# A hybrid convolution and state-space layer on one core: the last convolved tiles stay in SBUF, and the group norms are taken from four rows of 128

## The chip, the cores and the metric

The kernel runs on one core of one Trainium2 chip. The time is the device time of one execution in microseconds (us); several executions are timed and the median is given. The engines are PE (TensorE, matrix products), DVE (VectorE), ACT (ScalarE), POOL (GpSimd) and SP (SyncE, whose queue issues most DMAs; GpSimd and ACT issue DMAs on queues of their own). Each engine works through its instructions in a fixed order and waits on semaphores. The order is made when the kernel is built: a planner goes through the instructions with a priority for each (mainly its place in the program, shifted by hand with `tc.high_priority`) and with durations of its own, and writes one list for each engine.

## What is computed

One decoder layer on 1024 positions with 1024 channels, in float32. The part that matters here is the first sublayer, the mixers:

```python
h = layer_norm(x, ln_in_g, ln_in_b)
u = h @ w_in            # conformer GLU | z | x,B,C | dt | gate_a | gate_b
v = a * sigmoid(g);  v = causal_dwconv(v, 31 taps)        # conformer branch
y_a = silu(layer_norm(v)) @ w_conv_out
y   = SSD(silu(causal_dwconv(x,B,C)), dt) + x * d_skip     # Mamba-2 branch, 4 groups
yg  = y * silu(z)
yg  = yg * rsqrt(mean(yg**2 over the 512 channels of a group) + eps)
y_b = (yg * norm_w) @ w_ssm_out
h = layer_norm(alpha*h + (sigmoid(gate_a)*y_a + sigmoid(gate_b)*y_b) @ w_o)
h = layer_norm(alpha*h + conv_ffn(h))
```

Two normalisations are touched by the change: the norm over the 1024 channels of the convolved `v` (eight tiles of 128 channels), and the norm over the 512 channels of each of four groups of the state-space branch.

## The kernel before

Activations lie with channels on the 128 partitions and positions along the row. The sequence is worked in two halves of 512 positions, so a tile is 128 x 512. Float32 products are made from a high and a low part: a weight tile is loaded by SP into `st`, ACT casts the high part (L141), DVE subtracts to get the low part (L142), and each block takes three products (L153, L154, L155). One column of 128 channels is 8 blocks, 24 products (`project`). PSUM has eight banks, four (`acc`) for the projections and four (`sm`) for the rest.

For each half, `mixers` runs over four groups. For group g it projects the columns of B and C and four of x, each followed by a short convolution on DVE (`conv4`, L391); four z columns (`z_gate`); and two pairs of conformer columns (`glu`), which give two tiles `v`. Then `ssd_group` does the state-space part in four chunks of 128 positions: transposes (L478), decay factors on ACT (L485, L492), GpSimd's product `ce` (L496), products for the outputs (L517 and L520), the gate (L543), squares on ACT (L545), and DVE's sum of squares over the four tiles of a chunk into `ssum` (L546).

The function `scaled` makes the norm of one group: a product of `ssum` with a 128 x 128 matrix of ones (L553) gives every partition the sum over channels, ACT takes the square root (L554), DVE the reciprocal (L555) on 128 x 512, and four DVE instructions multiply `xT` by weight and norm (L558). The function `parts` splits the result into high and low parts in `yT` (L571 on ACT, L572 on DVE), which the output projection `ssm_out_first` (first half of the channels, eight columns) and the second half in `combine` use. The tiles `xT` have two buffers (`x4`), `ssum`, `rstd` and `ce` one each.

Meanwhile `conv31` convolves the two tiles `v` of the group with 31 taps: ACT starts each accumulator `c` (L425, two buffers), and DVE adds 30 taps to each, 60 instructions for a group (L436). It has a low priority (an offset of -1500), so its taps fill DVE wherever nothing more urgent is ready. Both accumulators then go to device memory (L445).

In the fourth group the first half of the output projection comes before the last splits. At the end of `mixers` eight gate columns are projected and stored. `combine` projects the other gates and the second half of the output projection (16 columns in turn), and, with a raised priority, does the conformer norm: SP loads the eight convolved tiles back (L655), GpSimd adds them (L660, L662), PE makes the mean by a product with a constant matrix (L664), then come differences (L667), squares (L669, L672), GpSimd's sum of these (L673), a second product (L675), and the normalised tiles for the last projection `wconv`. SP's queue holds the stores L445, the loads L655, the loads of the other branch `yb` (L643) and the weight loads (L139) in one line.

After `combine` of the second half come the output projection and the feed-forward part, about 700 us, which the change doesn't touch.

Of the kernel before, what the change touches and what calls it, by code (L numbers as in the profile page):

```python
# [55 lines left out]
def kernel(  # L56
# [31 lines left out]
    def bank(which):  # L88
        n_ps[0] += 1
        pl, tag = (pacc, "acc") if which else (psm, "sm")  # L90
        return pl.tile([P, 512], F32, tag=tag, name=f"{tag}{n_ps[0]}")
# [37 lines left out]
        [dram.tile([P, T], F32, name=f"{n}_scr{k}") for k in range(NK)] for n in ("b2", "t32")  # L129
    )  # L130
    acs_scr = [dram.tile([P, P], F32, name=f"acs_scr{i}") for i in range(2)]
    c_scr = [dram.tile([8, P, HALF], F32, name=f"c_scr{i}") for i in range(2)]
    g_scr = [dram.tile([8, P, HALF], F32, name=f"g_scr{i}") for i in range(2)]
    y_scr = [dram.tile([8, P, HALF], F32, name=f"y_scr{i}") for i in range(2)]
# [12 lines left out]
    def big_tile(name):  # L147
        return big.tile([P, 2, KD, HALF], F32R, tag="big", name=name)
# [255 lines left out]
    def glu(pl, hh, hT, i):  # L404
        pa, pg = bank(1), bank(1)
        wa = weights(wcol[CT_A + i], f"ga{hh}_{i}")
        project(pa, wa, hT)
        wg = weights(wcol[CT_G + i], f"gg{hh}_{i}")
        project(pg, wg, hT)
        v = pl.tile([P, HALF + KC - 1], F32, tag="v", bufs=4, name=f"v{hh}_{i}")  # L410
        s = pl.tile([P, HALF], F32, tag="sig", name=f"sig{hh}_{i}")
        A.activation(out=s, in_=pg, func=AF.Sigmoid)
        A.copy(v[:, : KC - 1], v_halo[:, i, :])
        V.tensor_mul(v[:, KC - 1 :], pa, s)
        if hh == 0:
            A.copy(v_halo[:, i, :], v[:, HALF:])
        return v

    def conv31(pl, hh, vs):

        accs = {}
        for i, v in vs:
            wc = PC_CW + i * KC
            c = pl.tile([P, HALF], F32, tag="c", bufs=2, name=f"c{hh}_{i}")
            A.activation(  # L425
                out=c,
                in_=v[:, KC - 1 :],
                func=AF.Identity,
                scale=pc[:, wc + KC - 1 : wc + KC],
                bias=pc[:, PC_CB + i : PC_CB + i + 1],  # L430
            )
            accs[i] = c
        for k in range(KC - 1):
            for i, v in vs:
                wc = PC_CW + i * KC
                V.scalar_tensor_tensor(  # L436
                    out=accs[i],
                    in0=v[:, k : k + HALF],
                    scalar=pc[:, wc + k : wc + k + 1],
                    in1=accs[i],  # L440
                    op0=ALU.mult,
                    op1=ALU.add,
                )
        for i, _ in vs:
            SY.dma_start(c_scr[hh][i], accs[i])  # L445

    def z_gate(pl, hh, hT, g):

# [5 lines left out]
    def ssd_group(pl, hh, g, xT, BT, CT, zs):  # L454
# [10 lines left out]
        for c in range(4):  # L465
# [67 lines left out]
            for i in range(4):  # L533
# [9 lines left out]
            V.tensor_mul(xT[:, :, cs], xT[:, :, cs], zs[:, :, cs])  # L543
            sq = pl.tile([P, 4, P], F32, tag="sq", name=f"sq{nm}")
            A.activation(out=sq, in_=xT[:, :, cs], func=AF.Square)  # L545
            V.tensor_reduce(  # L546
                out=ssum[:, cs], in_=sq.rearrange("p i l -> p l i"), axis=AX.X, op=ALU.add
            )

        def scaled():  # L550
            rstd = pl.tile([P, HALF], F32, tag="rstd", name=f"rstd{hh}_{g}")
            pv = bank(0)
            TE.matmul(pv, ones, ssum, start=True, stop=True)  # L553
            A.activation(out=rstd, in_=pv, func=AF.Sqrt, bias=eps, scale=1.0 / HALF)  # L554
            V.reciprocal(out=rstd, in_=rstd)  # L555
            for i in range(4):
                k = PC_NW + 4 * g + i
                V.scalar_tensor_tensor(  # L558
                    out=xT[:, i, :],
                    in0=xT[:, i, :],  # L560
                    scalar=pc[:, k : k + 1],
                    in1=rstd,
                    op0=ALU.mult,
                    op1=ALU.mult,
                )
# [12 lines left out]
    def ssm_out_first(pl, hh, yT):  # L578
        for j in range(8):
# [4 lines left out]
            A.copy(y, ps)  # L584
            SY.dma_start(y_scr[hh][j], y)

    def mixers(hh, hT):
        pre = first_columns(hh, hT, (CT_B, CT_C, CT_X))
        with pool(f"mixers{hh}") as pl:
            time_steps(pl, hh, pre[0])  # L590
            for g in range(GROUPS):
                BT = conv4(pl, hh, column(hh, hT, CT_B + g) if g else pre[1], 16 + g)
                CT = conv4(pl, hh, column(hh, hT, CT_C + g) if g else pre[2], 20 + g)
                xT = pl.tile([P, 4, HALF], F32, tag="x4", bufs=2, name=f"x4_{hh}_{g}")
                for i in range(4):
                    j = 4 * g + i
                    conv4(pl, hh, column(hh, hT, CT_X + j) if j else pre[3], j, xT[:, i, :])
                zs = z_gate(pl, hh, hT, g)
                vs = [(i, glu(pl, hh, hT, i)) for i in (2 * g, 2 * g + 1)]
                scaled, parts = ssd_group(pl, hh, g, xT, BT, CT, zs)  # L600
                if g == 2:
                    scaled()
                    split_2 = parts
                elif g == 3:
                    ssm_out_first(pl, hh, yT)
                    yT = big_tile(f"yT{hh}_{g}")
                    split_2(yT)
                    scaled()
                    parts(yT)
                else:  # L610
                    if g == 0:
                        yT = big_tile(f"yT{hh}_{g}")
                    scaled()
                    parts(yT)
                with tc.high_priority(offset=-1500):
                    conv31(pl, hh, vs)
            for j in range(8):
                pg = bank(1)
                project(pg, weights(wcol[CT_GA + j], f"gt{hh}_{j}"), hT)
                ga = pl.tile([P, HALF], F32, tag="ya", bufs=2, name=f"gt{hh}_{j}")  # L620
                A.activation(out=ga, in_=pg, func=AF.Sigmoid)
                SY.dma_start(g_scr[hh][j], ga)
        return yT

    def combine(hh, hT, yT):

        with pool(f"comb{hh}") as pl:
            mb, gbs = [], []
# [21 lines left out]
            with tc.high_priority(offset=900):  # L650
                cs = []
                for i in range(8):
                    if i % 2 == 0:
                        pair = pl.tile([P, 2, HALF], F32, tag=f"c{i // 2}", name=f"cc{hh}_{i}")
                    SY.dma_start(pair[:, i % 2, :], c_scr[hh][i])  # L655
                    cs.append(pair[:, i % 2, :])
# [462 lines left out]

    warm(75)  # L1120
    hT = ln_in_first()
    yT = mixers(0, hT)
    mixT, hT = combine(0, hT, yT)
    with pool("rows0") as pl:
        rs = [pl.tile([P, D], F32, name=f"r0_{t}") for t in range(4)]
        out_proj(pl, rs, 0, mixT)
        for t in range(4):
            SY.dma_start(h1_scr[t * P : (t + 1) * P, :], rs[t])
    yT = mixers(1, hT)
    state_stack.close()  # L1130
    mixT, _ = combine(1, hT, yT)
    ffn_stack = ExitStack()
    qp = ffn_stack.enter_context(pool("ffq", side="right"))
    with pool("trans") as tp:
# [118 lines left out]
```

## Time and profile before

| | us |
|---|---|
| median of three runs | 2007.0 (2004.78 to 2007.89) |
| the profiled execution | 2003.94 |
| its span, from the first to the last instruction | 2001.9 |
| PE busy | 1938.3 |
| DVE busy | 1697.2 |
| ACT busy | 1088.9 |
| GpSimd busy | 199.2 |

Busy time of PE counts products from start to modelled end, and since these overlap, a busy PE isn't always one that advances at its best rate. A wait in the views is the idle time of one engine in front of an instruction, put down to the engine or DMA that ended it. Tiles are named as in the program, without buffer numbers; `acc` and `sm` are PSUM banks.

### The profile page before, as it was taken

The numbers are of one execution on the slowest core, as the hardware profiler recorded it, in microseconds if no ns is written. First come the engines' busy times: TensorE is split into PE (matmuls) and PEld (weight loads), VectorE is DVE, ScalarE is ACT, GpSimd is POOL, SyncE is SP. The second block draws the span as 40 slices with busy tenths as digits, with TensorE's granted clock in tenths as the row PEclk, the third lists the DMA queues.
The fourth block names the chain that finished last, engine by engine and source line by source line (L and its number), as shares of the span: only waits on it lengthen the run. The fifth ranks groups of instructions, "written<-read, shape, count | busy, mean of one in ns | idle before, by whom it ended". The sixth has DMA issues, their size and how long they took to land.

```text
span 2001.9 us, 25547 instructions
## 1 busy us (share of the span) xinstructions
PE 1938.3 (97%) x9405; PEld 1578.4 (79%) x9405; DVE 1697.2 (85%) x2256; ACT 1088.9 (54%) x1619; POOL 199.2 (10%) x230
## 2 busy tenths in 40 slices
PE   9999999999699999999999979999999999989997
PEld 8888888777588788887777768888888888868886
DVE  7599999999695669999999977578788888869778
ACT  4676768553263266776685426355555555544432
POOL 0001010110410000101011022001000000121010
PEclk9999999999899999999999999999999999999999
DMA  5333333334465432323234353476455555578663
GB/s 216 110 97 109 105 101 111 115 132 138 142 223 169 161 108 98 108 99 106 92 120 137 118 168 126 134 278 240 152 168 195 174 179 179 174 278 310 195 227 126
DMA packets 110237, 311.20 MB, mean 155 GB/s; under 512 B 12832, under 2 KB 13344, under 8 KB 110112
## 3 DMA queue, kind: packets, MB, share of 16 engines
q1 hardware_dynamic: 91872, 256.61, 38.4%
q0 software_dynamic: 11904, 41.43, 5.9%
q10 hardware_dynamic: 6336, 11.54, 1.6%
q8 instruction: 74, 1.21, 0.2%
q14 instruction: 51, 0.42, 0.1%
HBM read 255.39 MB, written 54.13 MB: 155 GB/s over the span
## 4 chain that ended last, share of the span: by engine, by line
PE 53%; DVE 32%; DMA 6%; issue 5%; ACT 2%; POOL 1%; SPq 0%; DVEq 0%; ACTq 0%; POOLq 0%
DVE c L436 12%; PE acc L155 11%; PE acc L154 11%; PE acc L153 11%; PE sm L154 5%; PE sm L155 5%; PE sm L153 5%; DVE w_c L142 2%; DVE x L391 2%; DMA dr<-wdown 2%; DVE w_dn L1041 1%; DVE m L512 1%; DMA dr<-b_scr 1%; DVE x L535 1%; DVE xbc L391 1%
## 5 line engine op out<-in xcount | busy, mean ns | idle before, releaser
L436 DVE SCALAR_TENSOR_TENSOR c<-v,pc,c 128x512 f32<-128x512 f32 x480 | 364.2, 792 | 3.6 <-ACT c L425 2.5
L153 PE MATMUL acc<-hT,w_c 128*128 128x512 f32 x616 | 241.3, 392 | 0.6 <-ACT w_c L141 0.6
L155 PE MATMUL acc<-hT,w_c 128*128 128x512 f32 x616 | 239.8, 391 | 1.0 <-DVE w_c L142 0.9
L154 PE MATMUL acc<-hT,w_c 128*128 128x512 f32 x616 | 240.6, 391 | 0.0
L496 POOL TENSOR_TENSOR ce<-ce,xbc 128x1024 f32<-128x1024 f32 x28 | 80.8, 2886 | 843.6 <-ACT ce L495 843.6
L153 PEld LDWEIGHTS acc<-hT,w_c 128*128 128x128 f32 x616 | 115.7, 188 | 26.0 <-ACT w_c L141 1.0
L155 PEld LDWEIGHTS acc<-hT,w_c 128*128 128x128 f32 x616 | 115.7, 188 | 25.7 <-DVE w_c L142 2.1
L154 PEld LDWEIGHTS acc<-hT,w_c 128*128 128x128 f32 x616 | 115.7, 188 | 23.5
L141 ACT CAST w_c<-st_c 128x1024 fp32r<-128x1024 f32 x80 | 83.9, 1048 | 81.3 <-PE acc L155 64.9
L142 DVE TENSOR_TENSOR w_c<-st_c,w_c 128x1024 fp32r<-128x1024 f32 x80 | 98.5, 1233 | 27.2 <-ACT w_c L141 27.0
L1040 ACT CAST w_dn<-dr 128x1024 fp32r<-128x1024 f32 (+1 forms) x73 | 68.7, 944 | 86.1 <-DVE dr L975 30.7
L485 ACT ACTIVATE m<-ab,acs 128x128 f32<-128x128 f32 x256 | 78.4, 390 | 51.4 <-PE sm L517 51.1
L153 PE MATMUL sm<-h1s,w_s 128*128 128x512 f32 x264 | 103.0, 390 | 0.0
L154 PE MATMUL sm<-h1s,w_s 128*128 128x512 f32 x264 | 102.9, 390 | 0.0
L155 PE MATMUL sm<-h1s,w_s 128*128 128x512 f32 x264 | 102.5, 390 | 0.0
L1041 DVE TENSOR_TENSOR w_dn<-dr,w_dn 128x1024 fp32r<-128x1024 f32 (+1 forms) x73 | 78.6, 1086 | 5.8 <-ACT w_dn L1040 5.8
L391 DVE SCALAR_TENSOR_TENSOR x<-u,pc,x 128x512 f32<-128x512 f32 x96 | 77.0, 813 | 0.0
L155 PE MATMUL acc<-h1b,w_ue 128*128 128x512 f32 x176 | 68.9, 395 | 0.3 <-DVE w_ue L142 0.2
L153 PE MATMUL acc<-h1b,w_ue 128*128 128x512 f32 x176 | 68.7, 390 | 0.0
L154 PE MATMUL acc<-h1b,w_ue 128*128 128x512 f32 x176 | 68.5, 389 | 0.0
L153 PE MATMUL sm<-h1b,w_s 128*128 128x512 f32 x176 | 68.5, 389 | 0.0
L154 PE MATMUL sm<-h1b,w_s 128*128 128x512 f32 x176 | 68.5, 389 | 0.0
(338 smaller groups left out, 5346.9 us busy)
## 6 DMA issues: line engine op xcount, KB each, us to landing
st_c<-wcol SPq DMA_DIRECT2D x80, 512.0 KB, 3.5
ab<-acs_scr SPq DMA_DIRECT2D x32, 512.0 KB, 4.0
dr<-wdown SPq DMA_DIRECT2D x55, 256.0 KB, 5.0
st_wo<-wo SPq DMA_DIRECT2D x24, 512.0 KB, 4.1
st_ue<-wup SPq DMA_DIRECT2D x22, 512.0 KB, 3.8
first_scr<-first ACTq DMA_DIRECT2D x44, 256.0 KB, 2.7
ra<-wup SPq DMA_DIRECT2D x22, 512.0 KB, 3.5
rb<-wup SPq DMA_DIRECT2D x22, 512.0 KB, 3.7
```

Of the source, the lines that this page charges most:

```text
L141: A.copy(w[:, 0, :], st)
L142: V.tensor_tensor(out=w[:, 1, :], in0=st, in1=w[:, 0, :].bitcast(F32), op=ALU.subtract)
L153: TE.matmul(ps, wa(0), xa(0), start=start, stop=False, skip_group_check=more)
L154: TE.matmul(ps, wa(0), xa(1), start=False, stop=False, skip_group_check=more)
L155: TE.matmul(ps, wa(1), xa(0), start=False, stop=stop, skip_group_check=more)
L391: V.scalar_tensor_tensor(out=o, in0=u[:, k : k + HALF], scalar=pc[:, wc + k : wc + k + 1], in1=o, op0=ALU.mult, op1=ALU.add,)
L436: V.scalar_tensor_tensor(out=accs[i], in0=v[:, k : k + HALF], scalar=pc[:, wc + k : wc + k + 1], in1=accs[i], op0=ALU.mult, op1=ALU.add,)
L485: A.activation(out=m[:, h, :], in_=ab[:, h, :], func=AF.Relu, scale=-1.0, bias=acs[:, c, 8 * g + h : 8 * g + h + 1],)
L496: G.tensor_tensor(out=ce, in0=ce, in1=CT[:, cs].unsqueeze(1).to_broadcast([P, 8, P]), op=ALU.mult)
L512: V.tensor_tensor(out=m, in0=m, in1=cbm.unsqueeze(1).to_broadcast([P, 8, P]), op=ALU.mult)
L1040: A.copy(w[:, 0, cs], src)
L1041: V.tensor_tensor(out=w[:, 1, cs], in0=src, in1=w[:, 0, cs].bitcast(F32), op=ALU.subtract)
```

## The change

Two things are changed in the mixers and in `combine`.

The accumulators of `conv31` move from the pool of `mixers` to the pool `statep`, which stays open through `combine`. Only tiles 0 to 5 are stored; `conv31` returns the last two accumulators, and `combine` uses them in place instead of loading them. `state_stack` is closed after the second `combine` instead of before it.

The group norm changes its form and its place. The sum of squares over four tiles becomes two additions. The product with the ones becomes four products of 32 columns each, in four column tiles of PE, so that the sums over channels of the four chunks lie on four bands of 32 partitions, 128 positions in a row. Square root and reciprocal work on 128 x 128. GpSimd's queue stores one row of each band to device memory and loads the 512 values back to all partitions. And `scaled` and `parts` of group g are placed behind the columns of group g+1, ahead of its `ssd_group`; for the last group they come after three of the eight gate columns, which move ahead of the other five into `gate_first`.

```diff
+    nrm_scr = [dram.tile([4, P], F32, name=f"nrm_scr{i}") for i in range(2 * GROUPS)]
...
-            c = pl.tile([P, HALF], F32, tag="c", bufs=2, name=f"c{hh}_{i}")
+            c = statep.tile([P, HALF], F32, tag="c", bufs=2, name=f"c{hh}_{i}")
...
         for i, _ in vs:
-            SY.dma_start(c_scr[hh][i], accs[i])
+            if i < 6:
+                SY.dma_start(c_scr[hh][i], accs[i])
+        return accs
...
-            V.tensor_reduce(
-                out=ssum[:, cs], in_=sq.rearrange("p i l -> p l i"), axis=AX.X, op=ALU.add
-            )
+            V.tensor_add(sq[:, 0:2], sq[:, 0:2], sq[:, 2:4])
+            V.tensor_add(ssum[:, cs], sq[:, 0], sq[:, 1])
 
         def scaled():
             rstd = pl.tile([P, HALF], F32, tag="rstd", name=f"rstd{hh}_{g}")
+            rows = pl.tile([P, P], F32, tag="rows", name=f"rows{hh}_{g}")
             pv = bank(0)
-            TE.matmul(pv, ones, ssum, start=True, stop=True)
-            A.activation(out=rstd, in_=pv, func=AF.Sqrt, bias=eps, scale=1.0 / HALF)
-            V.reciprocal(out=rstd, in_=rstd)
+            for j in range(4):
+                TE.matmul(
+                    pv[j * HEADS : (j + 1) * HEADS, :P],
+                    ones[:, :HEADS],
+                    ssum[:, j * P : (j + 1) * P],
+                    start=True,
+                    stop=True,
+                    tile_position=(0, j * HEADS),
+                )
+            A.activation(out=rows, in_=pv[:, :P], func=AF.Sqrt, bias=eps, scale=1.0 / HALF)
+            V.reciprocal(out=rows, in_=rows)
+            scr = nrm_scr[hh * GROUPS + g]
+            G.dma_start(scr, rows.rearrange("(j r) l -> j r l", j=4)[:, 0, :])
+            G.dma_start(rstd, scr.rearrange("j l -> (j l)").partition_broadcast(P))
...
+    def gate_first(pl, hh, hT, js):
+        for j in js:
+            pg = bank(1)
+            project(pg, weights(wcol[CT_GA + j], f"gt{hh}_{j}"), hT)
+            ga = pl.tile([P, HALF], F32, tag="ya", bufs=2, name=f"gt{hh}_{j}")
+            A.activation(out=ga, in_=pg, func=AF.Sigmoid)
+            SY.dma_start(g_scr[hh][j], ga)
+
     def mixers(hh, hT):
...
+            scaled = parts = None
...
                 vs = [(i, glu(pl, hh, hT, i)) for i in (2 * g, 2 * g + 1)]
+                if g:
+                    scaled()
+                if g == 1:
+                    yT = big_tile(f"yT{hh}_0")
+                if g in (1, 2):
+                    parts(yT)
+                split_2 = parts
                 scaled, parts = ssd_group(pl, hh, g, xT, BT, CT, zs)
-                if g == 2:
-                    scaled()
-                    split_2 = parts
-                elif g == 3:
+                if g == 3:
                     ssm_out_first(pl, hh, yT)
-                    yT = big_tile(f"yT{hh}_{g}")
+                    yT = big_tile(f"yT{hh}_2")
                     split_2(yT)
-                    scaled()
-                    parts(yT)
-                else:
-                    if g == 0:
-                        yT = big_tile(f"yT{hh}_{g}")
+                    gate_first(pl, hh, hT, range(3))
                     scaled()
                     parts(yT)
                 with tc.high_priority(offset=-1500):
-                    conv31(pl, hh, vs)
-            for j in range(8):
...
-        return yT
+                    accs = conv31(pl, hh, vs)
+            gate_first(pl, hh, hT, range(3, 8))
+        return yT, accs
...
                 for i in range(8):
+                    if i in accs:
+                        cs.append(accs[i])
+                        continue
                     if i % 2 == 0:
                         pair = pl.tile([P, 2, HALF], F32, tag=f"c{i // 2}", name=f"cc{hh}_{i}")
                     SY.dma_start(pair[:, i % 2, :], c_scr[hh][i])
...
-    yT = mixers(1, hT)
+    yT, accs = mixers(1, hT)
+    mixT, _ = combine(1, hT, yT, accs)
     state_stack.close()
-    mixT, _ = combine(1, hT, yT)
```

More of the change, by code (lines that the diff above doesn't have):

```diff
@@ L615, in mixers, with combine @@
                 with tc.high_priority(offset=-1500):
-                    conv31(pl, hh, vs)
-            for j in range(8):
[L618 to L622, printed above, removed]
-        return yT
-    def combine(hh, hT, yT):
+                    accs = conv31(pl, hh, vs)
+            gate_first(pl, hh, hT, range(3, 8))
+        return yT, accs
+    def combine(hh, hT, yT, accs):
         with pool(f"comb{hh}") as pl:
@@ L1121 @@
     hT = ln_in_first()
-    yT = mixers(0, hT)
-    mixT, hT = combine(0, hT, yT)
+    yT, accs = mixers(0, hT)
+    mixT, hT = combine(0, hT, yT, accs)
     with pool("rows0") as pl:
```

## The prediction

> **What bounds the kernel now.** The page comes first: the busy line and the slices tell whether one engine carries the span and where it is let down.
>
> ```profile
> span 2001.9 us, 25547 instructions
> PE   9999999999699999999999979999999999989997
> DVE  7599999999695669999999977578788888869778
> ```
>
> PE is at work in nearly every slice of 50 us. It is let down in the eleventh (500 to 550 us) and the twenty-fourth (1150 to 1200), the ends of the two mixers stages, and in the last. In the mixers stages DVE is as full as PE. Second, the waits of PE, with the total, the number and the longest:
>
> ```profile
> PE sm L664 <- POOL stats L662: 23.4, 2, 14.5
> PE sm L517 <- DVE m L512: 5.3, 6, 1.4
> PE sm L553 <- DVE ssum L546: 4.8, 5, 2.1
> ```
>
> Two waits, one in each half of the sequence, make 23.4 us. L664 is the product for the mean of the conformer norm; it waits for GpSimd's sum over the eight convolved tiles. Third, busy time by stage: start and end, then PE, PEld, DVE, ACT and POOL busy, then the granted clock.
>
> ```profile
> 100.00:468.00 368.00, 364.30 (x1943) 293.59 (x1941) 366.90 (x513) 245.70 (x420) 30.77 (x11) 1.00 0.34 113
> 468.00:519.10 51.10, 49.39 (x214) 39.64 (x212) 50.24 (x64) 17.12 (x20) 0.00 (x0) 1.00 0.36 115
> 519.10:533.60 14.50, 0.01 (x1) 0.01 (x1) 4.13 (x5) 0.60 (x1) 9.72 (x7) 0.59 0.72 234
> 770.00:1137.00 367.00, 357.46 (x1952) 287.20 (x1950) 365.02 (x501) 249.26 (x396) 45.23 (x15) 1.00 0.33 110
> 1189.20:1198.10 8.90, 0.03 (x1) 0.00 (x0) 5.96 (x5) 0.60 (x1) 8.48 (x6) 0.78 0.44 146
> ```
>
> From 100 to 519.1 us DVE is busy 417.1 of 419.1 us and PE 413.7: two full engines side by side. Then PE stands for 14.5 us (8.9 in the second half). Fourth, the timeline around these stops, by engine (start, length, engine, line, group):
>
> ```profile
> 509.31 9.28 DVE L436 SCALAR_TENSOR_TENSOR c<-v,pc,c 128x512 f32<-128x512 f32 x12
> 510.08 8.86 SPq L445 DMA_DIRECT2D c_scr<-c  x2
> 519.00 3.77 SPq L655 DMA_DIRECT2D cc<-c_scr  x8
> 523.09 1.26 POOL L660 TENSOR_TENSOR stats<-cc 128x512 f32<-128x512 f32 x1 [79.90 <-DMA cc<-c_scr]
> 526.03 7.51 POOL L662 TENSOR_TENSOR stats<-stats,cc 128x512 f32<-128x512 f32 x5 [0.34 <-DMA cc<-c_scr]
> 533.59 1.22 PE L664 MATMUL sm<-stats,mean_w 128*128 128x512 f32 x1 [14.51 <-POOL stats L662]
> 1177.82 3.89 DVE L436 SCALAR_TENSOR_TENSOR c<-v,pc,c 128x512 f32<-128x512 f32 x5
> 1188.92 9.16 POOL L662 TENSOR_TENSOR stats<-stats,cc 128x512 f32<-128x512 f32 x6
> ```
>
> This is the chain to cut. DVE ends the last convolution (L436) at 518.59. SP, held at the store of that tile since 510.08, stores it and loads all eight tiles back, and GpSimd adds them one by one until 533.54: 15.0 us from the last tap to L664. In the second half it is 1181.71 to 1198.08, 16.4 us. PE has gate and output projections left that need none of this, but each engine's order is fixed when the kernel is built, and L664 stands among them. So the bound is **PE, with a late DVE and a long tail behind it** at two places.
>
> **The change, part by part.**
>
> *Last two tiles kept on chip.* Tiles 6 and 7 are used where DVE left them; tiles 0 to 5 were stored one or more groups earlier and can be loaded and summed beforehand. Behind the last tap stay two GpSimd additions. From the rows above one takes 7.51/5 = 1.50 or 9.16/6 = 1.53 us, so 3.0 us take the place of 15.0 and 16.4. SP loses four stores and four loads, and no longer stands for 8.9 us with loads behind it.
>
> *Less DVE work ahead of it.*
>
> ```profile
> L555 DVE RECIPROCAL rstd<-rstd 128x512 f32<-128x512 f32 x8 | 26.7, 3343 | 1.0 <-ACT rstd L554 1.0
> L293 DVE RECIPROCAL sp<-sp 128x128 f32<-128x128 f32 x2 | 1.9, 949 | 0.0
> L546 DVE TENSOR_REDUCE ssum<-sq 128x128 f32<-128x512 f32 x32 | 33.7, 1054 | 0.0
> L300 DVE TENSOR_TENSOR sp<-sp 128x128 f32<-128x128 f32 x12 | 3.5, 288 | 0.2
> L543 DVE TENSOR_TENSOR x<-x,zs 128x512 f32<-128x512 f32 x32 | 22.8, 711 | 0.0
> ```
>
> Eight reciprocals go from 3343 to 949 ns, the row of the same operation on 128x128: 8 x 2.39 = 19.2 us. 32 reductions of 1054 ns become two additions: 288 ns for 128 elements, and for 256, which no row shows, between 288 and 711, by the line through both 429 ns. 32 x (1054 - 717) = 10.8 us. Together 30.0 us, 15.0 for each half, off an engine that ends the stage. If nothing else moved, the mean would be ready at 518.6 - 15.0 + 3.0 = 506.6, and PE comes to L664 at 519.1; in the second half 1169.7 against 1189.2. But the order is planned anew, and the planner will put L664 earlier once the tail is shorter. So I don't take the whole 23.4: the nearest rows for a PE wait planned close behind DVE are L517 and L553, at most 2.1 us each. I leave 2.1 at each place: **-19.2 us** (ends 0 and -23.4).
>
> *The clock behind the stop.*
>
> ```profile
> 533.60:538.90 5.30, 5.30 (x11) 3.50 (x12) 5.30 (x8) 1.83 (x3) 1.17 (x1) 0.50 0.51 169
> 1198.10:1201.00 2.90, 2.87 (x5) 1.65 (x6) 2.42 (x4) 0.04 (x1) 0.00 (x0) 0.50 0.60 184
> ```
>
> After each stop PE works 5.3 and 2.9 us at a granted clock of 0.50, which loses half of that, 4.1 us. Within the first stop the mean is 0.59: (0.59 - 0.50)/0.50 x 14.5 = 2.6 us passed before the clock fell. A rest of 2.1 us stays below this: **-4.1 us** (ends 0 and -4.1).
>
> *The norm's product behind the next columns.* L553 waits 4.8 us for the sum of squares, five times. Moved behind the next group's projections it comes when the sum is long done; in the last group it stands behind the first half of the output projection and three gates: **-4.8 us** (end 0). The waits of L517 (5.3) may shrink with a lighter DVE; I take nothing and keep -5.3 as an end.
>
> *The product itself.* The moving data shrink from 512 to 128 columns, in four column tiles of 32.
>
> ```profile
> 212.55 0.39 PE L153 MATMUL acc<-hT,w_c 128*128 128x512 f32 x1
> 186.40 1.02 PE L553 MATMUL sm<-ssum,ones 128*128 128x512 f32 x2
> 213.10 1.09 PE L517 MATMUL sm<-m,xs 128*64 128x128 f32 x16
> 680.78 3.64 PE L351 MATMUL acc<-hT,st_dt 128*32 128x512 f32 x32
> ```
>
> Each product makes two records. A product's record of 0.39 us outlasts the step to the next (0.227, from the row of 550 to 600 us further down: 220 in 50 us) by 0.16; without this tail L553's pair takes 0.86 us. L351, in the same four tiles, needs 3.64/4 = 0.91 us for eight records of 512 columns: the four run side by side, so 128 columns would take 0.23. L517, tiles with 128 columns, needs 1.09/16 = 0.07 for a record, eight make 0.55. I take 0.55, the row with the same columns: 8 x 0.31 = **-2.5 us** (end -5.0). The Trainium skill (TensorEngine Tiling (Array Packing), Key Properties) says that a change of tiling mode drains the array first. By that rule, 16 changes (into the tiles and out, eight times) with an exposed tail of 0.16 us each, an estimate from the row of L153, would cost 2.6 us, and this term would be nothing; no row here isolates such a change.
>
> *What is added: a round trip through device memory.* GpSimd's queue stores 4 rows of 128 and loads them back to all partitions.
>
> ```profile
> acs_scr<-sp_rows SPq DMA_DIRECT2D x2, 64.0 KB, 1.6
> do<-t_scr POOLq DMA_DIRECT2D x11, 256.0 KB, 4.0
> ACT ce L495 <- DMA ab<-acs_scr: 6.4, 4, 3.5
> ab<-acs_scr SPq DMA_DIRECT2D x32, 512.0 KB, 4.0
> ```
>
> A small store lands after 1.6 us and a 256 KB load from GpSimd's queue after 4.0, so 5.6 us a norm. Against 2.4 us off the reciprocal, the chain from product to scaled tile grows by 3.2 us. On GpSimd the load waits for the store and the store for DVE; behind them stand the products ce (L496), for which PE's L520 waits. On DVE the scaling waits for the load; behind it stand convolution taps and the low parts of weights. If every norm held PE, that is 8 x 3.2 = 25.6 us; if the next columns cover it, nothing. The nearest row is the 32 broadcast loads of ab in the same stage: their readers lost 6.4 us in all, 0.2 each. At 0.2 for 16 transfers: **+3.4 us** (ends 0 and 25.6).
>
> *At nothing:* the shorter square root (ACT has 245.70 of 368 us busy), the buffers of c held longer, and the six loads moved ahead of the last taps, for which DMA (0.36 busy from 468 to 519) has room; without that room the six additions, 9 us, come back behind the taps, and the mean is at 515.6, still ahead of 519.1.
>
> Sum: -19.2 - 4.1 - 4.8 - 2.5 + 3.4 = **-27.2 us**. The profiled execution took 2003.9 us (span 2001.9) and becomes 1976.7; the median of the runs is 2007.0, 3.1 above it, and becomes 1979.8.
>
> **The rivals.**
>
> *The stop stays, only earlier.* The planner decides L664's place from its own durations. If DVE runs behind the plan by as much as now, PE meets L664 earlier and waits as long. For it: PE came to L664 14.5 us before its data, so the plan was wrong by that much. Against it: L553 waited at most 2.1 us at any place, so DVE alone wasn't that late before; the error lies largely in the tail that is cut. Time: only -4.8 - 2.5 + 3.4 = -3.9, so 2003.
>
> *Slower: the buffer of the group before last.* xT has two buffers, so the projections of group g+2 write where group g still waits for its norm.
>
> ```profile
> 205.61 1.22 DVE L572 TENSOR_TENSOR yT<-x,yT 128x1024 fp32r<-128x1024 f32 x1
> 212.15 0.69 ACT L389 ACTIVATE x<-acc,pc 128x512 f32<-128x512 f32 x1
> 203.22 0.68 DVE L414 TENSOR_TENSOR v<-acc,sig 128x512 f32<-128x512 f32 x1
> ```
>
> Now group 0 lets its buffer go at 206.8 and group 2 writes first at 212.15. Behind the columns of group 1 the norm starts near 203.9 instead of 186.4, and is 3.2 us longer: free at 206.8 + 17.5 + 3.2 = 227.5, 15.3 us after it is wanted. ACT would hold there, the banks of projections fill and PE stops; four such places (0 to 2 and 1 to 3, in two halves) cost up to 61 us, the time is 2007 - 27 + 61 = 2041. Against it: the planner can run the four z columns of the next group first (24 products of 0.227 us each, 5.45 us a column, 21.8 us in all). It turns slower from 27.2/4 = 6.8 us uncovered at each place.
>
> *The round trip is on the path.* All 25.6 us count: -27.2 + 22.2 = -5.0, so 2002. The Trainium skill (SBUF — State Buffer, Who interferes with whom) says that a DMA from GpSimd's queue can be starved of its descriptors while DVE holds a port that both share, and DVE is full here. The nearest rows speak against a large effect:
>
> ```profile
> L262 POOL DMA_DIRECT2D x<-x x4: 537/538/540, 566.9 to 576.7; - x4
> DMA to landing us min/median/max: 3.8/4.9/5.0
> 550.00:600.00 50.00, 50.00 (x220) 41.08 (x219) 45.30 (x62) 31.64 (x40) 5.47 (x10) 1.00 0.64 222
> ```
>
> With DVE busy 45.3 of 50 us, four loads of 512 KB were issued in 0.54 us each and landed within 5.0.
>
> **How the numbers follow.** Forecast case 0.65, from 1964 (every end: -23.4 - 4.1 - 4.8 - 5.0 - 5.3 = -42.6) to about 1994 (half of the stop left). The stop stays: 0.15, about 2003. The round trip on the path: 0.08, about 2002. The buffer: 0.12, 2011 to 2041. About 0.2%, 4 us, is what a measurement of this kernel can tell from no change, so "the same" is 2003 to 2011. Half of the two middle rivals falls there: faster 0.65 + 0.12 = 0.77, same 0.11, slower 0.12. The range leaves out the buffer case and the last few hundredths below: 1966 to 2009.
>
> **What would show it.** PE's wait at L664 under 3 us in both halves, and no granted clock under 1.00 near 520 and 1190; the last tap some 15 us earlier relative to PE; reciprocals at 0.95 us and no reduction of 1.05; no PE wait for ssum. Against it: a long wait at L664 with the two additions ready late; PE waits for ACT at the projections of groups 2 and 3 with xT as the reason; DVE idle in front of the scaling with a DMA as releaser; PE's L520 waiting for GpSimd.

## The result and the profile after

| | before | after |
|---|---|---|
| median of four runs each, us | 2005.89 (2003.0 to 2007.89) | 1972.62 (1969.84 to 1975.4) |
| ratio, 95% interval | | 0.9835, 0.9815 to 0.9856 |
| span of the profiled execution, us | 2001.9 | 1968.1 |
| last convolution tap ends, first and second half, us | 518.6, 1181.7 | 504.4, 1156.0 |
| product for the mean starts, us | 533.6, 1198.1 | 519.1, 1169.7 |
| first product of the second half, us | 680.8 | 662.0 |
| first product of the feed-forward part, us | 1346.3 | 1316.6 |

The changed kernel is 33.3 us faster; 27.2 were forecast. Of the 33.8 us between the spans, by the last two rows of the table, 18.8 come from the first half, 10.9 from the second, and 4.1 from the 650 us behind them, whose code is unchanged. Lines of the changed kernel are numbered a little higher: L557 is the norm's product (before L553), L566 the reciprocal (L555), L437 a tap (L436), L676 a load of a convolved tile (L655), L681 and L683 GpSimd's additions (L660, L662), L685 the product for the mean (L664).

The page of the changed kernel, its totals and the busy tenths of PE and DVE in 40 slices:

```profile
span 1968.1 us, 25694 instructions
...
PE 1933.7 (98%) x9453; PEld 1575.4 (80%) x9453; DVE 1668.7 (85%) x2288; ACT 1074.7 (55%) x1610; POOL 203.9 (10%) x246
...
PE   9999999999999999999999999999999999999997
...
DVE  7599999999795659999999986587788888879778
```

The two dips of PE have gone. PE's own work fell by 4.6 us (1938.3 to 1933.7); its idle time fell from 63.6 to 34.4 us, which is 29.2 of the 33.8. DVE's work fell by 28.5 us (1697.2 to 1668.7). PE's waits say which idle time went (what PE waited for: total, number of times, longest):

```profile
PE sm L520 <- DVE m L515: 4.8, 3, 2.9
PE acc L156 <- DVE w_c L143: 3.7, 3, 1.8
PE acc L155 <- DVE w_dn L1062: 2.2, 2, 1.3
PE sm L685 <- POOL stats L683: 2.1, 1, 2.1
PE sm L557 <- DVE ssum L550: 1.8, 2, 1.2
```

The stop at the product for the mean has gone from 23.4 us to 2.1, all of them in the first half; in the second PE doesn't wait there. In a second execution of this kernel the stop is 3.3 us, in two pieces. The wait for the sum of squares went from 4.8 to 1.8. The busy times by stage, with the columns of the prediction's windows (PE, PEld, DVE, ACT, POOL, granted clock, DMA share, GB/s):

```profile
100.00:468.00 368.00, 368.00 (x1984) 296.03 (x1983) 362.12 (x549) 245.23 (x421) 34.16 (x19) 1.00 0.35 117
468.00:519.00 51.00, 47.35 (x208) 38.56 (x206) 41.82 (x52) 14.53 (x18) 11.01 (x8) 1.00 0.53 171
770.00:1137.00 367.00, 355.62 (x1939) 285.88 (x1938) 358.82 (x519) 236.11 (x374) 42.23 (x22) 1.00 0.35 115
```

DVE is still full up to 468 us (362.12 of 368), so the taps still take whatever it has left. But just ahead of the product for the mean it now has 9.2 of 51 us to spare, where it had 0.9 of 51.1: it finished its taps with time in hand. And the tail behind the last tap? The timeline around it (start, length, engine, line, group):

```profile
502.88 1.53 DVE L437 SCALAR_TENSOR_TENSOR c<-v,pc,c 128x512 f32<-128x512 f32 x2
502.99 0.33 SPq L140 DMA_DIRECT2D st_gb<-wcol  x1
503.36 2.80 SPq L676 DMA_DIRECT2D cc<-c_scr  x6
...
508.06 1.29 POOL L681 TENSOR_TENSOR stats<-cc 128x512 f32<-128x512 f32 x1 [22.10 <-DMA cc<-c_scr]
509.43 5.72 POOL L683 TENSOR_TENSOR stats<-stats,cc 128x512 f32<-128x512 f32 x4
515.23 3.81 POOL L683 TENSOR_TENSOR stats<-stats,c 128x512 f32<-128x512 f32 x2
```

The last tap ends at 504.4 us, the sum at 519.04: 14.7 us, as long as before (15.0). Tiles 0 to 5 were not loaded beforehand. SP issues their loads at 503.36, one microsecond before the last tap ends, right behind a weight load (st_gb). GpSimd's first addition waits for them until 508.06, and GpSimd adds all eight tiles after that. In the second half it is 13.7 us (1156.0 to 1169.7). **The stop went mainly because the taps end sooner; the tail is hardly shorter.** What shows that, and which part of the change it came from, was the matter of the experiments.

### The profile page after: what moved, and what is told of

Read it like the earlier page. It is cut to its first block, busy times and chain, and to the rows that moved or that the text cites. A ratio compares the mean times of both kernels' runs of the same rounds, so it can differ in the third digit from the quotient of the medians.

```text
span 1968.1 us, 25694 instructions
## 1 busy us (share of the span) xinstructions
PE 1933.7 (98%) x9453; PEld 1575.4 (80%) x9453; DVE 1668.7 (85%) x2288; ACT 1074.7 (55%) x1610; POOL 203.9 (10%) x246
## 5 line engine op out<-in xcount | busy, mean ns | idle before, releaser
L437 DVE SCALAR_TENSOR_TENSOR c<-v,pc,c 128x512 f32<-128x512 f32 x480 | 363.2, 788 | 2.9 <-ACT c L426 1.9
L499 POOL TENSOR_TENSOR ce<-ce,xbc 128x1024 f32<-128x1024 f32 x28 | 74.2, 2652 | 714.3 <-ACT ce L498 714.3
L155 PEld LDWEIGHTS acc<-hT,w_c 128*128 128x128 f32 x616 | 115.7, 188 | 23.4
L143 DVE TENSOR_TENSOR w_c<-st_c,w_c 128x1024 fp32r<-128x1024 f32 x80 | 97.1, 1216 | 25.9 <-ACT w_c L142 25.7
```

Of the source, the lines that this page charges most:

```text
L143: V.tensor_tensor(out=w[:, 1, :], in0=st, in1=w[:, 0, :].bitcast(F32), op=ALU.subtract)
L155: TE.matmul(ps, wa(0), xa(1), start=False, stop=False, skip_group_check=more)
L437: V.scalar_tensor_tensor(out=accs[i], in0=v[:, k : k + HALF], scalar=pc[:, wc + k : wc + k + 1], in1=accs[i], op0=ALU.mult, op1=ALU.add,)
L499: G.tensor_tensor(out=ce, in0=ce, in1=CT[:, cs].unsqueeze(1).to_broadcast([P, 8, P]), op=ALU.mult)
```

## The experiments

Each ratio is against the kernel before, run beside it on the same chip; its median was 2004.1 us for the first four, 2002.3 for the next four and 2003.9 for the last four.

**The kept tiles alone.** The kernel before, with only the first part of the change:

```diff
-            c = pl.tile([P, HALF], F32, tag="c", bufs=2, name=f"c{hh}_{i}")
+            c = statep.tile([P, HALF], F32, tag="c", bufs=2, name=f"c{hh}_{i}")
...
-            SY.dma_start(c_scr[hh][i], accs[i])
+            if i < 6:
+                SY.dma_start(c_scr[hh][i], accs[i])
+        return accs
...
+                    if i in accs:
+                        cs.append(accs[i])
+                        continue
```

> The kernel before with only the last two convolved tiles kept on chip. Relief theory (the gain comes from DVE ending its taps earlier, since in the changed kernel 14.7 us still pass from the last tap at 504.4 to the mean's product at 519.1, against 15.0 before): the last tap stays near 518, PE still waits at least 10 and 6 us at the mean's product, the time falls by 0 to 4 us. Keep theory (the shorter tail is the gain, as the prediction had it): the wait falls under 4 us at both places and the time by 14 to 20 us.

Measured: 1993.07 us, ratio 0.9945 (0.993 to 0.996), 11 us faster. Its timeline at the end of the first half:

```profile
510.12 2.79 SPq L660 DMA_DIRECT2D cc<-c_scr  x6
...
523.18 3.39 POOL L667 TENSOR_TENSOR stats<-stats,c 128x512 f32<-128x512 f32 x2
```

and of its waits of PE:

```profile
PE sm L669 <- POOL stats L667: 11.0, 2, 5.7
```

Here the step does what the prediction said, in one half: the loads go out 13.5 us ahead of the last tap (523.6), and the mean starts 3.0 us behind it, at 526.6. In the second half they go out at 1170.7, behind a weight load again, and the tail is 12.5 us (1174.05 to 1186.57). The taps themselves did not come earlier in the first half (523.6, before 518.6), so half of the stop stayed (11.0 of 23.4). The 240 taps of that half took 187.4 us of DVE here and 181.7 before. The run lies between the two expectations and bears out neither: a short tail is worth something here, but far from the whole.

**All but the kept tiles.** The changed kernel with that part undone (the diff above, with the signs turned):

> The changed kernel with all eight convolved tiles stored and loaded again. Relief theory: the last tap stays near 504, the tail is 14 to 17 us, PE waits 2 to 6 us at the mean's product, the time is within 6 us of 1972.6. Keep theory: the wait grows by 12 us at both places and the time to 1985 or more.

Measured: 1981.75 us, ratio 0.9889 (0.9872 to 0.9905), some 9 us slower than the changed kernel (11 by the ratios). The tails are 16.9 and 18.3 us (505.1 to 522.0, 1164.5 to 1182.8), and the wait at the mean is this:

```profile
PE sm L680 <- POOL stats L678: 10.5, 2, 7.4
```

So the kept tiles do pay in the changed kernel, 8.4 us less wait at the mean, though they take only 2.2 and 4.6 us off the tails and not the 12 that were the reason given for them. Again the run lies between the two expectations.

**The new form of the norm alone, at its old place.** The kernel before, with the two additions for the reduction, the column tiles, the rows of 128 and the round trip; `scaled` and `parts` are called where they were:

```diff
-            V.tensor_reduce(
-                out=ssum[:, cs], in_=sq.rearrange("p i l -> p l i"), axis=AX.X, op=ALU.add
-            )
+            V.tensor_add(sq[:, 0:2], sq[:, 0:2], sq[:, 2:4])
+            V.tensor_add(ssum[:, cs], sq[:, 0], sq[:, 1])
...
-            V.reciprocal(out=rstd, in_=rstd)
+            V.reciprocal(out=rows, in_=rows)
+            scr = nrm_scr[hh * GROUPS + g]
+            G.dma_start(scr, rows.rearrange("(j r) l -> j r l", j=4)[:, 0, :])
+            G.dma_start(rstd, scr.rearrange("j l -> (j l)").partition_broadcast(P))
```

> The kernel before with only the new form of the group norm (two additions, column tiles, 128x128 root and reciprocal, round trip through device memory), at its old place. Relief theory: 15 us of DVE work less in each half, the last tap 12 to 16 us earlier, the time 20 to 30 us lower. If the round trip needs the new place to hide, DVE waits for it by more than 2 us a norm (16 us in all) and the time falls by less than 12 us.

Measured: 1970.83 us, ratio 0.9834 (0.9819 to 0.9849): **the whole gain, with no tile kept and no norm moved**, and more than the 20 to 30 us expected. All eight tiles go through device memory here, and the tails are as long as ever (505.3 to 520.9 and 1149.8 to 1169.7), yet the waits are small (of PE at the mean, and of DVE's scaling for the loaded norm):

```profile
PE sm L676 <- POOL stats L674: 3.9, 2, 3.5
```

```profile
DVE x L570 <- DMA rstd<-nrm_scr: 2.8, 4, 1.6
```

The taps end 13.3 and 31.9 us earlier than before (13.8 of the 31.9 because the second half begins earlier, at 667.0 us), and PE reaches the mean with its sum nearly ready.

**The new place alone.** The kernel before, with `scaled` and `parts` behind the next group's columns and three gates ahead, and the norm in its old form:

```diff
+                if g:
+                    scaled()
+                if g == 1:
+                    yT = big_tile(f"yT{hh}_0")
+                if g in (1, 2):
+                    parts(yT)
...
+                    gate_first(pl, hh, hT, range(3))
                     scaled()
                     parts(yT)
```

> The kernel before with only the new place of the norms and gates. Both theories: the waits for ssum (4.8 us) go and the rest stays, the waits at the mean's product too, so 2 to 8 us lower. If the buffer of the group before last is missed (the slower rival of the prediction), 5 us or more slower.

Measured: 2002.21 us, ratio 0.9989 (0.9978 to 1.0). PE's wait for the sum of squares goes from 4.8 to 1.8 us as in the changed kernel, and the stop stays:

```profile
PE sm L668 <- POOL stats L666: 22.2, 2, 13.6
```

Moved by itself, the norm brings at most 0.2%.

**The two halves of the new form.** Both are the kernel before with one of them: the rows of 128 with column tiles and round trip, and the old reduction; or the two additions alone (parts of the diff above).

> The kernel before with the norm in rows (column tiles, 128x128 root and reciprocal, round trip) but the old reduction over four tiles. DVE is lightened by 19.2 us instead of 27. Relief in proportion: 19.2/27.2 of 33 us, so 20 to 26 us lower than before. If the reductions were the part that counts: less than 12 us lower.

> The kernel before with only the two additions in place of the reduction. DVE is lightened by 8 us (33.7 to 25.7 in the changed kernel). Relief in proportion: 6 to 12 us lower. If the form of the norm is what counts: 0 to 4 us lower.

Measured: the rows 1985.35 us, ratio 0.9904 (0.9882 to 0.9925); the additions 1993.84 us, ratio 0.9945 (0.992 to 0.9969). The waits at the mean, of the kernel with the rows:

```profile
PE sm L677 <- POOL stats L675: 10.2, 1, 10.2
```

and of the kernel with the additions:

```profile
PE sm L663 <- POOL stats L661: 19.7, 2, 12.0
```

In the row of four (before, additions, rows, both) the last tap of the first half ends at 518.6, 514.9, 509.6 and 505.3 us, that of the second at 1181.7, 1169.5, 1165.4 and 1149.8, and the stop is 23.4, 19.7, 10.2 and 3.9 us. Of the shift in the second half 3.6, 6.9 and 13.8 us are its earlier start. In this row, the more DVE time is saved, the earlier the taps end and the shorter the stop. The additions gain what was expected, the rows less (20 to 26 us were). Apart, the additions gain 8.5 us and the rows 17.0, together 33.2 and not 25.5. The stop accounts for 2.6 of the 7.7 us between (19.5 less together, 3.7 and 13.2 apart); the rest was not followed up.

**The new norm with the kept tiles, at the old place.** The third kernel above with the diff of the first:

> The new form of the norm and the last two tiles kept on chip, at the old place: the changed kernel without its new place. Relief theory (with DVE lightened, PE's stop at the mean's product is down to 3.9 us in e3_norm_only, so keeping has almost nothing left to remove): 1965 to 1971, up to 6 us under e3_norm_only. Adding theory (each part brings what it brought alone, 11 and 33 us): 1960. Rival: keeping moves the planner's order as in e1_keep_only, where the last tap came 5 us later, and gives 3 us or more back: 1974 or more.

Measured: 1967.23 us, ratio 0.9815 (0.9792 to 0.9839). With the second run of it further down it is the fastest version. Over the norm alone it is 3.6 us lower, but the intervals overlap (0.9819 to 0.9849 there), so with the norm in its new form and old place a gain from the kept tiles is not clear of the noise.

**The sum taken as the tiles come.** The same with GpSimd adding each pair of tiles as soon as its taps end:

```diff
+        i, j = (i for i, _ in vs)
+        if i == 0:
+            c_sum[hh] = statep.tile([P, HALF], F32, tag="csum", name=f"csum{hh}")
+            G.tensor_add(c_sum[hh], accs[0], accs[1])
+        else:
+            for k in (i, j):
+                G.tensor_add(c_sum[hh], c_sum[hh], accs[k])
...
-                mean = stats[:, 0, :]
-                G.tensor_add(mean, cs[0], cs[1])
-                for c in cs[2:]:
-                    G.tensor_add(mean, mean, c)
+                mean = c_sum[hh]
```

> As e5_norm_keep, and the sum of the convolved tiles is taken by GpSimd as each pair ends, so that two additions stay behind the last tap. If the stop at the mean's product is only a matter of the tail: no wait there in either half, tail 3 to 4 us, and up to 5 us under e5_norm_keep. If the tail no longer sets anything: the same as e5_norm_keep within 3 us. If GpSimd's additions beside a full DVE cost DVE time (its taps took 2.8 us beside ce): 2 us or more above it.

Measured: 1968.54 us, ratio 0.982 (0.9799 to 0.9841), the same as without it. The sum needs no load any more, and PE's waits list none at the mean. PE's product for the mean in the first half:

```profile
510.54 1.02 PE L687 MATMUL sm<-csum,mean_w 128*128 128x512 f32 x2
```

That is 6.8 us behind the last tap (503.8), and in the second half 6.0 us (1148.9 to 1154.9), where the same kernel without the early sum has 15.8 and 16.2. So here the tail did become short, in both halves, and it brought nothing: only 2.6 us of the stop had been left. Once the taps end early, the tail's length doesn't set the time.

**The gates back.** The second kernel above, with all eight gate columns behind the last norm again:

```diff
-                    gate_first(pl, hh, hT, range(3))
                     scaled()
                     parts(yT)
...
-            gate_first(pl, hh, hT, range(3, 8))
+            gate_first(pl, hh, hT, range(8))
```

> e2_all_but_keep (new norm at the new place, no kept tiles) with all eight gate columns back at the end. e2_all_but_keep is 11 us above e3_norm_only, which differs by the place alone. If the later norms cost this (DVE waited 12.7 us for the round trip there, 2.8 in e3_norm_only, and PE's stop at the mean was 10.5 against 3.9): 1978 to 1985. If the three gates moved ahead cost it: 1969 to 1975.

Measured: 1981.73 us, ratio 0.988 (0.986 to 0.9901), against 1981.75 with three gates ahead. Between it and the kernel with the norm alone (1970.83) lies only where the norms of groups 0 to 2 are called, so that place costs some 9 to 11 us when the norm is new (ratios 0.988 and 0.9834). PE's stop at the mean is 7.0 us, against 3.9. Its taps end at 504.1 and 1159.8 us, 10 us later in the second half than at the old place, and DVE's scaling stands longer for the norm than the 2.8 us there:

```profile
DVE x L570 <- DMA rstd<-nrm_scr: 11.5, 6, 3.0
```

**A spare reciprocal.** To load DVE again without any other change, the kernel with the norm alone got eight reciprocals that nothing reads:

```diff
             V.reciprocal(out=rows, in_=rows)
+            spare = pl.tile([P, 3, P], F32, tag="spare", name=f"spare{hh}_{g}")
+            V.reciprocal(out=spare, in_=ones.unsqueeze(1).to_broadcast([P, 3, P]))
```

> e3_norm_only with a spare reciprocal of 128x384 on DVE behind each reciprocal, for which nothing waits: some 2.5 us each, 20 us in all, about what the rows took off DVE. Relief theory (only DVE's time ahead of the last tap counts): most of the 33 us go but the tree's share stays, 1987 to 1997, with PE's wait at the mean's product back at 12 us or more. Rival (the new form gains by its product on PE, its shorter root and its earlier start): 1976 or less.

Measured: 1971.81 us, ratio 0.9843 (0.9817 to 0.987), as without them. But the run tells nothing about the question. They read only a constant, and so the planner was free to set all eight where DVE had nothing to do (source view: minimum, median and maximum in ns, first and last start in us):

```profile
L566 DVE RECIPROCAL spare<-ones x8: 2543/2548/2554, 28.2 to 702.8; 128x384 f32<-128x384 f32 x8
```

The last of them starts at 702.8 us, ahead of the second half's norms, and the last taps came at 507.3 and 1149.4 us, against 505.3 and 1149.8 without them. The load was not where it should have been.

**The changed kernel and the best one, side by side**, both unchanged from above:

> The changed kernel once more, beside e12_norm_keep_again on the same chip: 1968 to 1975. If the new place costs something even with the kept tiles, 2 to 6 us above e12_norm_keep_again; if not, within 2 us of it.

> The kernel of e5_norm_keep (new norm and kept tiles, old place) once more: 1964 to 1971, 2 to 6 us under e11_changed_again if the new place costs something even with the kept tiles.

Measured: the changed kernel 1970.77 us, ratio 0.9848 (0.9822 to 0.9873); the new norm with kept tiles at the old place 1964.40 us, ratio 0.9808 (0.9788 to 0.9828). The intervals just overlap, but the order is that of the earlier runs (0.9835 and 0.9815). By the two pairs of ratios the move behind the next columns gives away some 4 to 8 us beside the kept tiles. Overlapping intervals don't settle that alone; without the kept tiles the loss is clear (0.986 to 0.9901 against 0.9819 to 0.9849). The move is better left out. In the best version the two waits of interest are these, of PE and of DVE:

```profile
PE sm L681 <- POOL stats L679: 0.8, 1, 0.8
```

```profile
DVE x L572 <- DMA rstd<-nrm_scr: 3.1, 4, 1.6
```

## Why the prediction was right, and which step failed

| term | forecast, us | in the changed kernel |
|---|---|---|
| stop at the product for the mean | -19.2 | -21.3 |
| clock behind it | -4.1 | -2.4: no half clock near 520 or 1170 us, but 3.4 us of it near 1061, which lose 1.7 |
| wait for the sum of squares | -4.8 | -3.0 |
| the product in column tiles | -2.5 | about nothing (below) |
| round trip | +3.4 | 11.2 on DVE, on PE not seen apart |
| waits for low parts of `w_c` | not named | +2.8 (0.9 to 3.7) |

The direction and the largest term came out: the stop left 2.1 us, where two rests of 2.1 were allowed for. **The reason given for the tail did not hold.** The step that failed is "tiles 0 to 5 were stored one or more groups earlier and can be loaded and summed beforehand", with 3.0 us in place of 15.0 and 16.4. They could be, and in the first half of the kernel with the kept tiles alone they were; in the changed kernel the loads left SP too late, and the tail took 14.7 and 13.7 us. The prediction's case for it, the mean at 515.6 "still ahead of 519.1", is the one that came, and it was 3.5 us too hopeful: the taps ended at 504.4 instead of 503.6, and it left out the time until the loads landed (503.36 to 508.06). PE was still not there before 517.0. Why SP's loads stand where they do, whether the buffer of a weight load ahead of them or the planner's own date holds them, isn't settled. The forecast of the stop survived because it didn't need this step: by the prediction's own sums the relief of 15.0 us with the old tail gives 503.6 + 15.0 = 518.6, just ahead of 519.1.

The other half of the argument carried the change. DVE was to be relieved of 30.0 us and was of 28.5. The groups of the changed kernel (count, busy time and mean ns of one, then idle time in front):

```profile
L549 DVE TENSOR_TENSOR sq<-sq 128x256 f32<-128x256 f32 x32 | 16.8, 524 | 2.7 <-ACT sq L548 2.7
...
L550 DVE TENSOR_TENSOR ssum<-sq 128x128 f32<-128x128 f32 x32 | 8.9, 279 | 0.0
...
L566 DVE RECIPROCAL rows<-rows 128x128 f32<-128x128 f32 x8 | 7.5, 940 | 0.0
```

The reciprocal is 940 ns (949 was taken). The two additions take 25.7 us in place of 33.7, 8.0 less and not 10.8, because two of the wide ones lasted 2.2 us (below). The runs with one part each show that this relief goes with earlier taps and a shorter stop, step by step. In the first half the traces show the size as well. There all of the norms' sums of squares and reciprocals lie ahead of the last tap, in each of these kernels. They take 30.3 us of DVE before, and 5.7, 9.4 and 15.3 us less with the additions, the rows and both; the last tap comes 3.7, 9.0 and 13.3 us earlier. In the kernel with the kept tiles alone they take as long as before, the taps themselves 5.7 us longer, and the last comes 5.1 us later. So the end of the taps follows the DVE work ahead of it. What no run does is to put the same work back in the same place; the spare reciprocals were to do it and did not. In that one respect the cause is argued, not shown.

Smaller terms. The wait for the sum of squares was to go and left 1.8 us; the new place alone leaves the same 1.8, but the kernel with the new norm at the old place has 1.2, so the move was not needed for it. The waits for `m` were taken at nothing and went from 5.3 to 4.8. Of the 4.1 us behind the feed-forward's first product, 3.6 are idle time of PE (18.9 to 15.3 us), most of it waits for the parts of `w_dn` (7.3 to 4.1). Why these shrink with the same code isn't known. That part takes between 650.8 us (the new norm with kept tiles) and 657.4 (the additions alone), and 651.5 and 653.2 in two executions of the changed kernel. Without it the change is worth 29.7 us.

The product in column tiles gained nothing, where 2.5 us were forecast. In the changed kernel its 64 records come in 13 visits to the tiles and not 8, because the planner laid transposes or projections between some of them. One visit with six records:

```profile
449.60 0.39 PE L156 MATMUL acc<-hT,w_gt 128*128 128x512 f32 x1
449.92 0.42 PE L557 MATMUL sm<-ssum,ones 128*32 128x128 f32 x6
450.27 0.50 PE L154 MATMUL acc<-hT,w_gt 128*128 128x512 f32 x1
450.60 0.39 PE L155 MATMUL acc<-hT,w_gt 128*128 128x512 f32 x1
```

From the product ahead of it to the second one behind it pass 1.00 us, and without two ordinary steps of 0.227 us the visit costs 0.55. One with two records (456.62 us) costs 0.54 by the same count, so nearly all of this is the price of a visit, whatever it holds. The undivided product cost 0.87 (at 186.40 us in the kernel before). 13 visits make 7.1 us and eight undivided products 6.9, estimates from these rows. The prediction's second price for the term, nothing, is the one that came. With the norm alone there are 21 visits, so that kernel's gain doesn't come from this product.

The term for the round trip holds a slip: 16 transfers at 0.2 us are 3.2 us, not 3.4. And that the sum came so near is partly luck. Beside the stop, -8.0 us were forecast. Up to the feed-forward part -8.4 came (29.7 less 21.3), but from other places: -2.4 from the clock, -3.0 from the sum of squares, nothing from the product, -0.5 from the waits for `m`, +2.8 from `w_c`, -3.5 from waits that were not named, and -1.8 that these rows don't place.

The rivals. "The stop stays, only earlier" is out in the changed kernel, and is just what the move alone showed (22.2 of 23.4 us left). The buffer of the group before last didn't bite: neither ACT nor PE has a wait for a buffer of `xT`, and no group's projections stop. The round trip was issued in 0.59 and 0.57 us and landed as forecast: from issue to landing (minimum, median, maximum; first the store, then the load),

```profile
DMA to landing us min/median/max: 1.6/2.0/3.5
```

```profile
DMA to landing us min/median/max: 3.6/4.3/4.7
```

so 6.1 to 8.7 us pass from the end of a reciprocal to the first scaling. By the Trainium skill (SBUF — State Buffer, Who interferes with whom) GpSimd's DMAs could have been starved beside a busy DVE; with DVE at 362 of 368 us no issue here was held up. PE had no wait for `ce`, which stands behind these transfers on GpSimd. DVE did stand for the loaded norm:

```profile
DVE x L572 <- DMA rstd<-nrm_scr: 11.2, 6, 3.0
```

That is 11.2 us in the changed kernel and 2.8 to 5.2 with the norm at the old place. So a part of this rival was real, on DVE, and it came with the place that was to cover it; what stands in front of the scaling in the one order and not in the other was not traced.

## What to carry to other kernels

Where two full engines run side by side up to a point at which one waits for the other, shorten the work of the late one first: here 28 us off DVE took away a stop that looked like the fault of a long tail behind it. Run each part of a change alone before they are combined: one part carried the whole gain, one helped a little, and the third, meant as cover for the new round trip, cost time together with it though it was harmless by itself. And spare work for an experiment needs an input that is made in the stage under test, or the planner lays it where it hurts nobody.

## What the hardware showed beside this

DVE's wide additions and taps, which read two tiles in SBUF, are held when they begin inside one of GpSimd's products (`ce`, L499). The source view of the wide addition in the changed kernel (ns, minimum, median, maximum), and the timeline of DVE and GpSimd at its longest:

```profile
L549 DVE TENSOR_TENSOR sq<-sq x32: 407/412/2209, 126.2 to 1109.0; 128x256 f32<-128x256 f32 x32
```

```profile
370.06 2.40 POOL L499 TENSOR_TENSOR ce<-ce,xbc 128x1024 f32<-128x1024 f32 x1 [20.14 <-ACT ce L498]
...
370.53 2.21 DVE L549 TENSOR_TENSOR sq<-sq 128x256 f32<-128x256 f32 x1 [0.88 <-ACT sq L548]
```

The addition began 0.47 us into GpSimd's product and lasted 0.28 us beyond its end. Of the 32, two overlap a product on GpSimd and took 2203 and 2209 ns; the other thirty took 407 to 426. Of the 480 taps, 13 begin inside such a product; they took 1851 to 2894 ns and ended 0.55 us behind it, each of them. The eight that were under way when GpSimd's product began took 732 to 752, as the other 459 did (median 741, none over 756). The 29 instructions of L538 that begin inside one, and have one of their two tiles in PSUM, took 329 to 343 ns, as elsewhere (median 334). The Trainium skill (SBUF — State Buffer, Who interferes with whom) says that a DVE instruction with two SBUF inputs contends with GpSimd's reads; the trace agrees, and the price is the rest of GpSimd's instruction. For the taps that is some 23 us on the engine that was late; taking the products away from GpSimd was not tried.

A short rest of PE was enough for the lower clock: in the changed kernel PE stands for 2.94 us from 1057.5 us on, and the next 3.4 us run at half clock (windows, columns as above):

```profile
1057.50:1060.90 3.40, 0.51 (x10) 0.54 (x12) 3.40 (x5) 1.24 (x2) 0.00 (x0) 1.00 0.13 28
1060.90:1064.30 3.40, 3.40 (x29) 2.83 (x25) 3.40 (x7) 1.06 (x4) 0.00 (x0) 0.50 0.65 217
```

The granted clock is 1.00 in the window of the rest and 0.50 in the one behind it, where 29 products take the 3.40 us. The rest of 2.1 us at the mean had no such sequel (1.00 throughout). The prediction's bound for a rest without loss, 2.6 us, fits both, but other runs don't keep to it. With the gates back, a rest of 2.25 us was followed by half clock; in the kernel with all but the kept tiles, one of 3.05 us was not:

```profile
1175.96:1178.21 2.25, 0.00 (x1) 0.00 (x1) 1.07 (x1) 0.00 (x0) 2.12 (x1) 1.00 0.15 54
1178.80:1182.10 3.30, 3.30 (x8) 2.27 (x7) 2.28 (x4) 0.96 (x2) 0.00 (x0) 0.50 0.27 107
```

```profile
1179.72:1182.77 3.05, 0.00 (x1) 0.01 (x1) 1.87 (x1) 0.00 (x0) 2.92 (x2) 1.00 0.30 99
1182.77:1190.00 7.23, 7.23 (x30) 5.67 (x31) 6.07 (x10) 3.69 (x6) 3.00 (x3) 1.00 0.17 65
```

So a rest's length alone doesn't tell whether the clock falls, and that 2.1 us went without loss was partly luck.
